# LP pooling in one dimension: one square and one sum per load, one root per store, and the small piece loaded second

## The chip, the cores and the metric

One core of a Trainium2 chip. ACT (ScalarE), DVE (VectorE) and SP (SyncE) are engines of the core that compute or issue transfers; 16 DMA engines move the data. The metric is the device time of one execution in microseconds (us). A kernel is compared by its runs in the same rounds on the same chip.

## The reference

```python
# x: 32 x 256 x 4096 float32, p = 2, kernel_size = 4
for i in range(out_length):                       # 1024
    window = np.abs(x[:, :, i*4:i*4+4]) ** p
    result[:, :, i] = (np.mean(window, axis=-1)) ** (1.0 / p)
```

With p = 2 this is a square, a sum over four neighbours, and a root with scale 1/4. The core reads 134.22 MB and writes 33.55 MB.

## The kernel before

x is taken as one flat array. 22 loads (18 of 13184 float32 columns on 128 partitions, then smaller ones) go into three slots, buffers that are used in turn. ACT squares each chunk in place, DVE sums groups of four, ACT takes the root, and a store follows for each group of loads. 840 columns per partition do not fit in this scheme. They form the **small piece**, 107,520 elements laid over 120 partitions, kept in a buffer that is not needed until later. A load is issued on SP's DMA queue as soon as its slot is free. The stores of groups 0 to 6 are issued on ACT's queue, those of groups 7 to 10 on SP's at the end.

```python
W, O_W = 13184, 6592
X_SLOTS, O_SLOTS = 3, 2
slots = [[(W, [4416, 4384, 4384])]] * 18          # width of a load, its chunks
slots += [[(6592, [3296, 3296])] * 2, [(6592, [3296, 3296]), (4216, [2112, 2104])]]
ODD = 840
groups = [2] * 9 + [3, 1]                         # loads to a store
FINE, ENDS, LAG = range(22), (), 1                # a root after every chunk
PAIRS = 16                                        # from this load on: packed adds
...
def total_sum(o, v, i):
    if i < PAIRS:
        nc.vector.tensor_reduce(out=o, in_=v.rearrange("p (n j) -> p n j", j=k), ...)
        return
    ...                                           # two adds: pairs, then pairs of pairs
    nc.vector.tensor_tensor(out=h, in0=q[:, :, 0:2], in1=q[:, :, 2:4], op=add)
    nc.vector.tensor_tensor(out=o, in0=h[:, :, 0], in1=h[:, :, 1], op=add)

Q = 120
odd = ODD * P // Q                                # 896 columns on 120 partitions
t = o_tiles[1][0:Q, 0:odd]
nc.sync.dma_start(out=t, in_=xf[(total - ODD) * P:total * P].rearrange("(p w) -> p w", p=Q))
...                                               # then loads 0, 1, 2
nc.scalar.activation(out=t, in_=t, func=Act.Square)
nc.vector.tensor_reduce(out=o, in_=..., op=mybir.AluOpType.add)
nc.scalar.activation(out=o, in_=o, func=Act.Sqrt, scale=1.0 / k)
nc.scalar.dma_start(out=of[...], in_=o)           # the small piece's store
...
for i in range(n):                                # for each chunk of each load:
    ...                                           # ACT squares, DVE sums, ACT roots
```

## Time and profile before

| | before |
|---|---|
| time, median of 3 runs | 394.59 us (394.59 to 394.62) |
| span of the profiled run | 392.8 us |
| bytes moved | 167.79 MB |
| busy: DMA, ACT, DVE | all but the two ends, 74%, 69% |

The prediction below shows the lines of the page and reads them. Two lines more are needed, from the timeline of the kernel before (start, length, engine, line, operation, tile; in brackets the idle time of the engine and what ended it). They show when loads 0 and 1 landed, since ACT stood waiting for them:

```profile
20.36 7.63 ACT L143 ACTIVATE xt<-xt 128x4416 f32<-128x4416 f32 x2 [12.97 <-DMA xt<-in_x_dram]
36.00 3.88 ACT L143 ACTIVATE xt<-xt 128x4416 f32<-128x4416 f32 x1 [1.06 <-DMA xt<-in_x_dram]
```

They started squaring at 20.36 and 36.00 us, 15.6 us apart, which is what 6.75 MB take at 433 GB/s.

### The profile page before, as it was taken

What the parts mean: (1) busy time and instruction counts of PE and PEld (TensorE: products, weight loads), DVE (VectorE), ACT (ScalarE), POOL (GpSimd) and SP (SyncE); (2) the same over time, 40 slices, a digit from 0 to 9 for tenths busy, and PEclk for the clock granted to TensorE, in tenths of its full rate; (3) what the DMA queues carried; (4) which work ended last, traced back from release to release, by engine and by line L of the source; (5) the groups of instructions that cost most, each with busy time, mean ns of one, the idle gap of its engine ahead of it and who ended that gap; (6) DMA issues with size and microseconds to landing.
All of it is one profiled execution on the core that took longest, in us unless ns stands there. A gap on an engine that the chain in (4) does not pass through costs nothing.

```text
span 392.8 us, 341 instructions
## 1 busy us (share of the span) xinstructions
DVE 271.8 (69%) x77; ACT 292.5 (74%) x128; POOL 0.2 (0%) x4
## 2 busy tenths in 40 slices
DVE  1059989594959495949594959495949494778781
ACT  3088987776776777677867786868586859899990
POOL 0000000000000000000000000000000000000000
DMA  9999999999999989999999999999999999999997
GB/s 361 420 429 446 446 446 384 430 470 430 389 432 473 430 387 435 467 430 422 432 435 430 427 435 427 430 435 459 459 404 430 459 438 430 395 430 432 429 432 315
DMA packets 5024, 167.79 MB, mean 427 GB/s; under 512 B 558, under 2 KB 678, under 8 KB 926
## 3 DMA queue, kind: packets, MB, share of 16 engines
q1 hardware_dynamic: 3879, 144.04, 85.2%
q10 hardware_dynamic: 1143, 23.73, 14.0%
q14 instruction: 2, 0.02, 0.0%
HBM read 134.22 MB, written 33.55 MB: 427 GB/s over the span
## 4 chain that ended last, share of the span: by engine, by line
DMA 62%; ACT 21%; DVE 10%; issue 4%; SPq 0%; ACTq 0%
DMA xt<-in_x_dram 62%; ACT xt L143 17%; DVE ot L96 8%; ACT ot L89 3%; ACT xt L89 1%; DVE xt L105 1%; DVE xt L106 0%; ACTq L86 0%; SPq L80 0%; SPq L112 0%; ACTq L89 0%
## 5 line engine op out<-in xcount | busy, mean ns | idle before, releaser
L143 ACT ACTIVATE xt<-xt 128x4384 f32<-128x4384 f32 (+4 forms) x62 | 229.6, 3705 | 85.1 <-DMA xt<-in_x_dram 81.9
L96 DVE TENSOR_REDUCE ot<-xt 128x1096 f32<-128x4384 f32 (+1 forms) x48 | 227.0, 4731 | 90.1 <-ACT xt L143 89.8
L89 ACT ACTIVATE ot<-ot 128x1096 f32<-128x1096 f32 (+1 forms) x54 | 59.8, 1107 | 1.8 <-DVE ot L96 1.1
L105 DVE TENSOR_TENSOR xt<-xt 128x1648 f32<-128x1648 f32 (+4 forms) x14 | 28.4, 2032 | 16.0 <-ACT xt L143 16.0
L89 ACT ACTIVATE xt<-xt 128x824 f32<-128x824 f32 (+2 forms) x8 | 6.5, 817 | 1.9 <-DVE xt L106 1.9
L106 DVE TENSOR_TENSOR ot<-xt 128x1096 f32<-128x1096 f32 (+1 forms) x6 | 7.8, 1303 | 0.2
L106 DVE TENSOR_TENSOR xt<-xt 128x824 f32<-128x824 f32 (+2 forms) x8 | 7.5, 939 | 0.3
L119 DVE TENSOR_REDUCE ot<-ot 120x224 f32<-120x896 f32 x1 | 1.1, 1086 | 5.7 <-ACT ot L117 5.7
L117 ACT ACTIVATE ot<-ot 120x896 f32<-120x896 f32 x1 | 0.9, 949 | 2.7 <-DMA ot<-in_x_dram 2.7
L117 ACT ACT_TABLE_LOAD x1 | 1.3, 1283 | 0.7 <-PEq L174 0.7
L123 ACT ACT_TABLE_LOAD x1 | 1.3, 1283 | 0.0
L123 ACT ACTIVATE ot<-ot 120x224 f32<-120x224 f32 x1 | 0.4, 389 | 0.0
L174 POOL MEMSET const-bfloat16-1.0<- 128x1 bf16 x1 | 0.1, 101 | 0.0
L174 POOL MEMSET const-uint8-127<- 128x1 uint8 x1 | 0.1, 101 | 0.0
L174 POOL MEMSET const-float32-0.0<- 128x1 f32 x1 | 0.1, 99 | 0.2 <-issue 0.2
L174 POOL MEMSET const-float32-1.0<- 128x1 f32 x1 | 0.1, 99 | 0.0
## 6 DMA issues: line engine op xcount, KB each, us to landing
xt<-in_x_dram SPq DMA_DIRECT2D x18, 6592.0 KB, 39.9
out_dram<-ot ACTq DMA_DIRECT2D x7, 3296.0 KB, 27.6
xt<-in_x_dram SPq DMA_DIRECT2D x3, 3296.0 KB, 29.4
out_dram<-ot SPq DMA_DIRECT2D x2, 3296.0 KB, 30.0
out_dram<-xt SPq DMA_DIRECT2D x1, 2472.0 KB, 10.4
xt<-in_x_dram SPq DMA_DIRECT2D x1, 2108.0 KB, 26.8
out_dram<-xt SPq DMA_DIRECT2D x1, 527.0 KB, 7.1
ot<-in_x_dram SPq DMA_DIRECT2D x1, 420.0 KB, 4.0
```

The lines of the kernel that those rows point to most:

```text
L89: nc.scalar.activation(out=o, in_=o, func=Act.Sqrt, scale=1.0 / k)
L96: nc.vector.tensor_reduce(out=o, in_=v.rearrange("p (n j) -> p n j", j=k), axis=mybir.AxisListType.X, op=add,)
L105: nc.vector.tensor_tensor(out=h, in0=q[:, :, 0:2], in1=q[:, :, 2:4], op=add)
L106: nc.vector.tensor_tensor(out=o, in0=h[:, :, 0], in1=h[:, :, 1], op=add)
L117: nc.scalar.activation(out=t, in_=t, func=Act.Square)
L119: nc.vector.tensor_reduce(out=o, in_=t.rearrange("p (n j) -> p n j", j=k), axis=mybir.AxisListType.X, op=mybir.AluOpType.add,)
L123: nc.scalar.activation(out=o, in_=o, func=Act.Sqrt, scale=1.0 / k)
L143: nc.scalar.activation(out=v, in_=v, func=Act.Square)
L174: nc = _bacc.Bacc("TRN2", target_bir_lowering=False, num_devices=1)
```

## The change

It makes work coarser: one square and one reduction for a whole load, one root for a whole store, which saves the fixed part of many instructions (the three squares of a load took 11.57 us in the profile before). The packed adds (two `tensor_tensor` adds in place of one reduction) begin one load earlier. Load 0 is issued first, so that the main stream starts at once; the small piece follows it, is squared on DVE instead of ACT, and is stored on SP's queue. The core of the diff:

```diff
-    slots = [[(W, [4416, 4384, 4384])]] * 18
-    slots += [[(6592, [3296, 3296])] * 2, [(6592, [3296, 3296]), (4216, [2112, 2104])]]
+    slots = [[(W, [W])]] * 17 + [[(W, [6592, 6592])]]
+    slots += [[(6592, [6592]), (6592, [6592])], [(6592, [6592]), (4216, [2112, 2104])]]
-    FINE, ENDS, LAG = range(22), (), 1
-    PAIRS = 16
+    FINE, ENDS, LAG = (), {19}, 1
+    PAIRS = 15
...
+    load(0)
+    nc.sync.dma_start(
+        out=odd_x, in_=xf[(total - ODD) * P:total * P].rearrange("(p w) -> p w", p=Q),
+    )
+    ahead = 1
...
+    def odd_sum():
+        nc.vector.tensor_tensor(out=odd_x, in0=odd_x, in1=odd_x, op=mybir.AluOpType.mult)
+        nc.vector.tensor_reduce(out=odd_o, ...)
+    def odd_root():
+        nc.scalar.activation(out=odd_o, in_=odd_o, func=Act.Sqrt, scale=1.0 / k)
+        nc.sync.dma_start(out=of[...], in_=odd_o)
...
             nc.scalar.activation(out=v, in_=v, func=Act.Square)
+            if i == 0 and c == 0:
+                odd_sum()
             total_sum(ots[g][:, summed:summed + step // k], v, i)
...
+            if i == 0 and c == 0:
+                odd_root()
```

More of the change, by code (lines that the diff above doesn't have):

```diff
@@ L110 @@
     odd = ODD * P // Q
-    t = o_tiles[1][0:Q, 0:odd]
-    nc.sync.dma_start(out=t, in_=xf[(total - ODD) * P:total * P].rearrange("(p w) -> p w", p=Q))
-    ahead = 0
+    odd_x = o_tiles[1][0:Q, 0:odd]
+    odd_o = o_tiles[1][0:Q, odd:odd + odd // k]
+    load(0)
[3 more added lines that the diff above has]
+    ahead = 1
     while ahead < n and loads[ahead][0] < X_SLOTS:
@@ L116 @@
         ahead += 1
-    nc.scalar.activation(out=t, in_=t, func=Act.Square)
-    o = o_tiles[1][0:Q, odd:odd + odd // k]
-    nc.vector.tensor_reduce(
-        out=o, in_=t.rearrange("p (n j) -> p n j", j=k),
-        axis=mybir.AxisListType.X, op=mybir.AluOpType.add,
-    )
-    nc.scalar.activation(out=o, in_=o, func=Act.Sqrt, scale=1.0 / k)
-    nc.scalar.dma_start(
-        out=of[(total - ODD) * P // k:total * P // k].rearrange("(p w) -> p w", p=Q), in_=o,
-    )
+    def odd_sum():
+        nc.vector.tensor_tensor(out=odd_x, in0=odd_x, in1=odd_x, op=mybir.AluOpType.mult)
+        nc.vector.tensor_reduce(
+            out=odd_o, in_=odd_x.rearrange("p (n j) -> p n j", j=k),
+            axis=mybir.AxisListType.X, op=mybir.AluOpType.add,
+        )
+    def odd_root():
+        nc.scalar.activation(out=odd_o, in_=odd_o, func=Act.Sqrt, scale=1.0 / k)
+        nc.sync.dma_start(
+            out=of[(total - ODD) * P // k:total * P // k].rearrange("(p w) -> p w", p=Q),
+            in_=odd_o,
+        )
     pending = []
```

## The prediction

> **What bounds the kernel now.** I read the page first: the slices in part 2, the costliest groups in part 5, and the chain of waits in part 4; then the windows view, the groups kept apart by shape, the waits of the SP queue and the timeline of the two ends.
>
> The slices and totals of the page:
>
> ```profile
> span 392.8 us, 341 instructions
> DVE 271.8 (69%) x77; ACT 292.5 (74%) x128; POOL 0.2 (0%) x4
> ...
> DMA  9999999999999989999999999999999999999997
> GB/s 361 420 429 446 446 446 384 430 470 430 389 432 473 430 387 435 467 430 422 432 435 430 427 435 427 430 435 459 459 404 430 459 438 430 395 430 432 429 432 315
> DMA packets 5024, 167.79 MB, mean 427 GB/s; under 512 B 558, under 2 KB 678, under 8 KB 926
> ```
>
> No compute engine is over 74%, while every slice of the DMA row except the last is 8 or 9. The windows view (length, DVE, ACT and POOL busy, clock, DMA share, GB/s) makes this sharper:
>
> ```profile
> 0.00:6.00 6.00, 0.28 (x1) 2.53 (x3) 0.20 (x4) 1.00 0.91 327
> 66.00:380.00 314.00, 229.38 (x65) 243.33 (x105) 0.00 (x0) 1.00 1.00 433
> 380.00:388.00 8.00, 3.09 (x4) 3.26 (x4) 0.00 (x0) 1.00 1.01 434
> ```
>
> For 314 us the 16 DMA engines are busy 100% at 433 GB/s, and still while the last roots are computed. At 433 GB/s, 167.79 MB take 387.5 us, so of the span of 392.8 only 5.3 us are anything else: the start before the first byte, a slow first few us, and the landing of the last store. The time of 394.59 us is the span plus 1.8. Arithmetic matters only if it lets the transfer queues run dry. The chain of waits (DMA 62%, ACT 21%, DVE 10%) misleads here: it steps through an ACT or DVE instruction because a load's issue waits for a slot, but that load then stands in line behind other loads. Its landing takes 39.9 us (part 6) although its 6.75 MB need only 15.6 us at 433 GB/s.
>
> [...] The trace runs at 433 to 434[...], so I take 434 as the wall. [...] each load lands behind the one before, and the stores on the ACT queue take 27.6 us where 3.38 MB alone need 7.8. [...]
>
> **The change part by part.** The rows I extrapolate from, kept apart by shape (count | busy us, mean ns | idle before):
>
> ```profile
> L96 DVE TENSOR_REDUCE ot<-xt 128x1096 f32<-128x4384 f32 x32 | 151.0, 4719 | 6.3 <-ACT xt L143 6.0
> L143 ACT ACTIVATE xt<-xt 128x4384 f32<-128x4384 f32 x36 | 138.4, 3843 | 3.3 <-ACT ot L89 3.3
> L89 ACT ACTIVATE ot<-ot 128x1096 f32<-128x1096 f32 x36 | 39.7, 1103 | 0.2
> L105 DVE TENSOR_TENSOR xt<-xt 128x1648 f32<-128x1648 f32 x6 | 11.3, 1875 | 3.9 <-ACT xt L143 3.8
> L105 DVE TENSOR_TENSOR xt<-xt 128x2192 f32<-128x2192 f32 x4 | 9.8, 2442 | 3.9 <-ACT xt L143 3.9
> ```
>
> Bytes: none removed, none added. This part is worth 0.
>
> Work on the engines: the slope of the adds is (2442-1875)/(2192-1648) = 1.042 ns per element. One square of 13184 columns is 3.84 + 8800 x 0.833 ns = 11.2 us (three were 11.6); one reduction is 4.72 + 8800 x 1.042 ns = 13.9 us (three were 14.2); one root of 6592 columns is 1.10 + 5496 x 0.833 ns = 5.7 us (six were 6.6). ACT loses roughly 1.4 us per two loads and DVE 0.6, about 12 and 6 us over the kernel, all beside the transfers: worth 0. Load 15 now uses packed adds, 7.0 + 3.6 = 10.6 us: also 0.
>
> Depth of the pipeline: this is the cost. A slot used to be free 18.7 us after landing (51.58 to 70.31 in the chain), because the chunks' squares and sums overlap. Now square and sum of a whole load run in sequence, 11.2 + 13.9 = 25.1 us, so the next load of that slot is issued 6.4 us later. What it must beat is the landing of the two loads already queued: 2 x 15.6 = 31.2 us without a store, 38.9 with one (13.5 + 3.38 MB at 434). My count at the tightest place (loads counted from 0): load 1 lands at 36.0 (the square before it finished by 31), its square ends at 47.2, its sum at 61.1; load 4 is issued then, and load 3 drains until 67.2. About 6 us remain, later some 14. So no gap. DVE needs 13.9 us per load and ACT 11.2 + 5.7/2 = 14.0, both below 15.6 even with no stores.
>
> Stores: the root of a group now follows a whole square, so a store is issued 17 us after the even load lands instead of 5 (56.50 against 51.55). Its buffer is written again about 33 us after that (load 4's square ends near 101.7, the store is issued near 68.9); with 27 to 28 us to land, some 4 to 5 us remain.
>
> The head: before, SP issues the small piece at 0.73 and load 0 at 1.24; the piece lands at 4.72 and the first 6 us run at 327 GB/s instead of 434. With load 0 first the small rows lie between big ones; I estimate a gain of 0.3 to 0.8 us. Square and table load of the small piece move off ACT's start, where nothing waited. The small store on SP is held until about 31.7, and load 3 is not wanted before 43.9: 0.
>
> The tail. Before:
>
> ```profile
> 376.98 1.95 ACT L143 ACTIVATE xt<-xt 128x2112 f32<-128x2112 f32 x1
> 380.26 4.88 SPq L86 DMA_DIRECT2D out_dram<-xt  x2
> 384.15 0.64 ACT L89 ACTIVATE xt<-xt 128x526 f32<-128x526 f32 x1 [1.53 <-DVE xt L106]
> ```
>
> The last stores are issued at 380.26 and 384.81, and before them two full stores from SP end at 384.7. From load 17's landing at 340.6, chaining the new durations on ACT (two squares 11.3, square of 18 5.7, root 5.7, squares of 19 and 20 11.3, root 2.9, square 1.9, a wait of 0.7 for DVE, root 1.6) gives the second to last store at 381.5 and the last at about 386.4, so 1.2 and 1.6 us later. The transfers ahead end between 383 and 384, and an issue needs about 1 us to its first byte: it just fits. If load 16's square and root run past 340.6, it is 1.3 us later still and the queue is empty for up to 0.7 us. I charge 0.2.
>
> Sum: 394.59 + 0 - 0.5 (head) + 0.2 (tail) = 394.3; I say 394.3.
>
> **The rivals.**
> Rival 1, the whole-load latency starves the queue: if a slot is freed later than I count, each missed deadline idles all DMA engines. For it: slack of only 6 us at loads 3 and 4, and two output buffers with 4 to 5. Against: every duration is a short extrapolation along measured slopes, the wait would heal once stores lengthen the period to 38.9 us, and a one-time miss of 2 us would make 396 to 397. A miss in every period would be needed for over 402.
> Rival 2, the tail becomes the bound: the chunks in the last loads are twice as long, so the pipeline drains later. For it: ACT is nearly continuously busy from 340.6 on and the last two stores have under 1 us of slack. It would make 395 to 397.
> Rival 3, fewer instructions make it faster: 12 us of ACT and 6 of DVE are saved. Against: DMA is at 1.00 share of the time; the floor by bytes is 386.6 us at 434 plus about 2 at the front, 1.5 at the back and 1.8 outside the span, 392. So faster by over 2% (under 386.7) is ruled out by the bytes, unless the wall itself moves.
>
> **Range and chances.** The head's gain bounds the low side at about 393.3; a late tail and one small gap set the high side at 396.3. Over 2% slower needs about 8 us of empty queue, which only a recurring stall gives: 2%. Faster 1%, same 97%.
>
> **What would show it right or wrong.** In the changed profile: squares near 11.2 us, reductions near 13.9, roots near 5.7; SP's fourth load issued near 44 and its fifth near 61, both before the queue runs out; a DMA share of 1.00 at 433 from 6 to 380 us; first load landed near 19 instead of 20.3, and the third still near 51; last stores issued near 381.5 and 386.4. It is wrong if any window in the middle falls below 1.00, if DVE reductions wait for a store, or if the final store is issued after 389.

What is cut out of the prediction are figures and rules that no trace or run of this case shows. No term of its sum is cut: 394.59 - 0.5 (head) + 0.2 (tail) = 394.3 us. What stays rests on the trace of the kernel before. 434 GB/s is the rate of its window from 380 to 388 us, and the 314 us before that ran at 433; that this is a wall is the author's estimate. Loads 0, 1 and 2 landed one behind the other, at 20.34, 35.97 and 51.56 us. The 0.833 ns per element of ACT are (3843 - 1103) / (4384 - 1096) from the rows shown, and the 1.042 ns of the adds fit the reductions too: (4719 - 1086) / (4384 - 896), the 1086 ns being the small piece's. The "about 1 us" from an issue to its first byte is that of the small piece, issued at 0.73 us with its first row at 1.75; the last row of the run ends at 391.4 of 392.8 us, which are the "1.5 at the back". The gain at the head is an estimate from 327 against 434 GB/s; that large rows hide the cost of small ones was not shown.

## The result and the profile after

| | before | after |
|---|---|---|
| time, median of 6 runs | 394.61 us (394.59 to 394.63) | 395.66 us (395.55 to 396.12) |
| ratio, fast runs | | 1.0028 (95%: 1.0015 to 1.0041) |
| span of the profiled run | 392.8 us | 394.0 us |
| busy ACT, DVE | 292.5, 271.8 us | 280.9, 262.9 us |
| last load landed | 369.12 us | 370.26 us |
| last store landed | 391.91 us | 393.09 us |

A ratio is the mean time of one kernel's fast runs over that of the other's of the same rounds, so not quite the ratio of the medians. The time is the same within 2%, and about 1 us longer. ACT lost 11.6 us of work, about as foretold, and DVE 8.9, and it bought nothing. The totals and the slices of the page after:

```profile
span 394.0 us, 200 instructions
DVE 262.9 (67%) x35; ACT 280.9 (71%) x39; POOL 0.2 (0%) x4
...
DMA  8999999999999999999999999999999999999997
```

The groups kept apart by shape (count | busy us, mean ns | idle before, and what ended it) give the new durations:

```profile
L96 DVE TENSOR_REDUCE ot<-xt 128x3296 f32<-128x13184 f32 x15 | 208.3, 13886 | 78.9 <-ACT xt L152 78.9
L152 ACT ACTIVATE xt<-xt 128x13184 f32<-128x13184 f32 x17 | 190.2, 11190 | 102.4 <-DMA xt<-in_x_dram 100.7 <-ACT ot L89 1.7
L89 ACT ACTIVATE ot<-ot 128x6592 f32<-128x6592 f32 x9 | 51.1, 5681 | 0.0
```

11.19, 13.89 and 5.68 us: the extrapolation along the slopes was right to the rounding. DVE waits for squares (78.9 and 22.1 us) and for the small piece (22.0), and never for a store, so the two output buffers suffice. Now the windows (length, DVE, ACT and POOL busy, clock, DMA share, GB/s), first the middle and the last stores:

```profile
66.00:380.00 314.00, 226.27 (x27) 237.70 (x30) 0.00 (x0) 1.00 1.00 432
380.00:388.00 8.00, 4.85 (x5) 4.83 (x4) 0.00 (x0) 1.00 0.99 427
```

The DMA engines are never out of work. The 1.2 us must be somewhere the share does not show: the engines are busy, and slower. The landings tell where. The timeline of the kernel after:

```profile
20.13 11.19 ACT L152 ACTIVATE xt<-xt 128x13184 f32<-128x13184 f32 x1 [18.12 <-DMA xt<-in_x_dram]
...
37.39 11.19 ACT L152 ACTIVATE xt<-xt 128x13184 f32<-128x13184 f32 x1 [4.37 <-DMA xt<-in_x_dram]
...
45.26 70.48 SPq L80 DMA_DIRECT2D xt<-in_x_dram  x5
```

Load 0 lands 0.23 us sooner than before, although nothing is ahead of it now. Load 1 lands 1.39 us later, although the same bytes have been read by then. Load 3 is issued at 45.26 us, long before load 2 lands at 52.95, so no lateness of slots is in it. From here the shift stays: 1.40 us at load 2, 1.14 at the last load, 1.18 at the last store. So all of it arises between loads 0 and 1, where the small piece now lies. The windows of that stretch, before and after:

```profile
16.00:24.00 8.00, 0.00 (x0) 3.64 (x1) 0.00 (x0) 1.00 1.00 430
```

```profile
16.00:24.00 8.00, 1.94 (x2) 3.87 (x1) 0.00 (x0) 1.00 1.01 370
```

The same busy share, 1.00 and 1.01, but 370 GB/s instead of 430: (430 - 370) x 8 us is 480 KB, or 1.1 us at 433.

The trace also records every row that a DMA engine moved. The usual time of a 52,736-byte row is 1947 ns, 27.1 GB/s for an engine. I add up, over all rows of a stretch, the time beyond bytes at 27.1 GB/s and divide by 16 engines. This makes the table that the rest is read from (us; the last two columns are when the 16 engines finished the last store, on average and the latest):

| kernel | 0-8 | 8-26 | 54-80 | whole run | mean end | latest end |
|---|---|---|---|---|---|---|
| before | 0.94 | 0.08 | 0.49 | 2.47 | 390.58 | 391.41 |
| after | 0.83 | **1.29** | 0.06 | 3.35 | 391.44 | 392.58 |

0.88 us more of slow rows, and the engines end 0.86 us later on average. The remaining 0.3 us is one engine that ends 1.14 us behind the mean instead of 0.83.

### The profile page after: what moved, and what is told of

Its sections match the earlier page's. It is cut to its first block, busy times and chain, and to the rows that moved or that the text cites. A ratio compares the mean times of both kernels' runs of the same rounds, so it can differ in the third digit from the quotient of the medians.

```text
span 394.0 us, 200 instructions
## 1 busy us (share of the span) xinstructions
DVE 262.9 (67%) x35; ACT 280.9 (71%) x39; POOL 0.2 (0%) x4
## 4 chain that ended last, share of the span: by engine, by line
DMA 44%; ACT 29%; DVE 16%; issue 8%; another core or an unknown queue 1%; ACTq 0%; SPq 0%
DMA xt<-in_x_dram 44%; ACT xt L152 23%; DVE ot L96 14%; ACT ot L89 6%; DVE xt L105 1%; ACT xt L89 1%; DVE xt L106 1%; ACTq L86 0%; SPq L114 0%; SPq L80 0%; ACTq L89 0%
## 5 line engine op out<-in xcount | busy, mean ns | idle before, releaser
L152 ACT ACTIVATE xt<-xt 128x13184 f32<-128x13184 f32 (+3 forms) x24 | 222.2, 9272 | 103.1 <-DMA xt<-in_x_dram 101.4
L96 DVE TENSOR_REDUCE ot<-xt 128x3296 f32<-128x13184 f32 x15 | 208.3, 13886 | 78.9 <-ACT xt L152 78.9
L89 ACT ACTIVATE ot<-ot 128x6592 f32<-128x6592 f32 x9 | 51.1, 5681 | 0.0
L105 DVE TENSOR_TENSOR xt<-xt 128x3296 f32<-128x3296 f32 (+3 forms) x9 | 34.5, 3835 | 22.4 <-ACT xt L152 22.1
L123 DVE TENSOR_TENSOR ot<-ot 120x896 f32<-120x896 f32 x1 | 1.1, 1093 | 22.0 <-DMA ot<-in_x_dram 22.0
L106 DVE TENSOR_TENSOR ot<-xt 128x3296 f32<-128x3296 f32 (+1 forms) x4 | 10.9, 2733 | 0.1
L89 ACT ACTIVATE xt<-xt 128x3296 f32<-128x3296 f32 (+2 forms) x3 | 5.6, 1870 | 2.8 <-DVE xt L106 2.8
L106 DVE TENSOR_TENSOR xt<-xt 128x1648 f32<-128x1648 f32 (+2 forms) x5 | 7.0, 1409 | 0.2
L124 DVE TENSOR_REDUCE ot<-ot 120x224 f32<-120x896 f32 x1 | 1.1, 1086 | 0.0
## 6 DMA issues: line engine op xcount, KB each, us to landing
ot<-in_x_dram SPq DMA_DIRECT2D x1, 420.0 KB, 20.8
```

The costliest lines, as they stand in the source:

```text
L123: nc.vector.tensor_tensor(out=odd_x, in0=odd_x, in1=odd_x, op=mybir.AluOpType.mult)
L124: nc.vector.tensor_reduce(out=odd_o, in_=odd_x.rearrange("p (n j) -> p n j", j=k), axis=mybir.AxisListType.X, op=mybir.AluOpType.add,)
L152: nc.scalar.activation(out=v, in_=v, func=Act.Square)
```

## The experiments

Twelve kernels ran. Those of one group shared a chip and the runs of the kernel before.

**First group: is it the place of the small piece (theory A) or the coarse work (theory B)?** The kernel before took 394.69 us here.

*The piece in first place again, all else as changed:*

```diff
-    load(0)
     nc.sync.dma_start(out=odd_x, ...)
+    load(0)
```

> The changed kernel with one thing undone: the small piece is again loaded ahead of load 0 (its arithmetic and its store stay as changed). Theory A (the small rows behind a full load make every DMA engine start slowly a second time, and that alone costs the 1.1 us): 394.5 us +-0.2, ratio to the kernel before 0.9995 to 1.0005, load 1 lands near 36.0 us instead of 37.4. Theory B (whole-load squares and sums, later issues and later stores cost it, the place of the piece is innocent): stays at 395.5 to 395.8.

Measured: 394.61 us (394.19 to 395.55), ratio 1.0003 (0.9990 to 1.0016). Load 1 lands in time:

```profile
35.77 11.19 ACT L152 ACTIVATE xt<-xt 128x13184 f32<-128x13184 f32 x1 [2.69 <-DMA xt<-in_x_dram]
```

The coarse work is all there and the median is that of the kernel before: A's number, not B's. But the runs scatter over 1.4 us, where the kernel before scatters over 0.5, and two of the five (395.48 and 395.55) are as slow as B would have them, so B is not out; the last part comes back to it. The profiled one took 395.48: its slow rows sum to 2.48 us as before, its mean end is 390.62, but one engine ended at 392.11, 1.49 us behind.

*The kernel before, with load 0 ahead of the piece:*

```diff
-    nc.sync.dma_start(out=t, ...)
-    ahead = 0
+    load(0)
+    nc.sync.dma_start(out=t, ...)
+    ahead = 1
```

> The kernel before with one thing done: load 0 is issued ahead of the small piece; chunks, roots and sums as before. Theory A: 395.5 to 395.9 us, load 1 lands near 37.3. Theory B: stays at 394.6 +-0.1.

Measured: 395.51 us (395.24 to 396.53), ratio 1.0024 (1.0011 to 1.0038). Its window:

```profile
16.00:24.00 8.00, 0.00 (x0) 0.90 (x1) 0.00 (x0) 1.00 1.03 350
```

350 GB/s, 1.77 us of slow rows between 8 and 26 us, mean end 391.91 (the profiled run took 396.32 us; load 1 landed at 38.61, later than written). The order of two lines is enough to make the kernel before as slow as the changed one. (ACT's first square waits here for the piece until 23.1 us; load 3 is still issued at 44.81, before load 2 lands at 54.25.)

*The piece behind all three first loads:*

```diff
-    load(0)
-    nc.sync.dma_start(out=odd_x, ...)
-    ahead = 1
+    ahead = 0
     while ahead < n and loads[ahead][0] < X_SLOTS:
         load(ahead)
         ahead += 1
+    nc.sync.dma_start(out=odd_x, ...)
```

> The changed kernel with the small piece behind all three first loads instead of behind load 0. Theory A: the second slow start is merely moved, so 395.3 to 395.8 us again, with load 1 near 36 and load 2 near 51.5 us but load 3 late by 1 to 1.5 us. A variant of A, that it hurts only right behind the first load where the engines are still out of step: 394.4 to 394.6. Theory B: 395.6.

Measured: 415.47 us, ratio 1.0526. A fault of my edit, and a lesson: the piece's sum stands ahead of load 0's in DVE's program, so DVE waited 52.5 us for the piece while load 0 lay squared. No slot was freed, and the transfers ran dry:

```profile
52.00:70.00 18.00, 17.45 (x4) 15.23 (x3) 0.00 (x0) 1.00 0.16 47
```

47 GB/s instead of 433 for 18 us loses 16 of the 20.8 us. This run tells nothing of A and B, but it shows what a dry queue looks like, and that the changed kernel has none.

*No piece at all: its columns are added to the last load.*

```diff
-    slots += [..., [(6592, [6592]), (4216, [2112, 2104])]]
-    ODD = 840
+    slots += [..., [(6592, [6592]), (5056, [2528, 2528])]]
+    ODD = 0
```

(and the piece's instructions removed)

> The changed kernel without a small piece: its 840 columns a partition are added to the last load (5056 columns, two chunks of 2528), same bytes. Theory A: neither the small rows nor a second slow start remain, 393.6 to 394.3 us. Theory B: 395.2 to 395.6, as the coarse work is all still there. The last store should be issued near 387.6 us.

Measured: 395.58 us (395.26 to 395.85), ratio 1.0021. A miss for A's number. The stretch from 8 to 26 us is clean (0.01 us), as A says, but 0.86 us of slow rows turn up between 54 and 80 us, where the first store starts, against 0.49 before and 0.06 in the changed kernel; and one engine ended 1.56 us behind the mean. So taking the piece away removes its slow rows, and the time stays. The larger part of what takes their place is that engine: against the kernel before, the mean end is 0.16 us later and the latest end 0.88.

**Second group: what about the piece is slow?** The kernel before took 394.64 us here. A1: a run of small rows is slow by itself. A2: 15 of 16 engines get a share, and being out of step costs. (In the trace of the changed kernel 15 completions of the piece come from 20.17 to 22.01 us and one at 1.76, when the first row of load 0 only starts; load 0 on 128 partitions has 16 from 18.29 to 20.10.)

*128 partitions instead of 120, still second:*

```diff
-    Q = 120
+    Q = 128
```

> The changed kernel with the small piece on 128 partitions (rows of 3360 bytes, all 16 DMA engines) instead of 120 (3584 bytes, 15 engines), still in second place. Theory A1 (a run of small rows behind big ones is what costs, whoever carries it): 395.4 to 395.9 us, as the change. Theory A2 (the engine that gets no share of the piece runs ahead and the others pay for being out of step): 394.5 to 394.9.

Measured: 395.40 us (395.11 to 395.61), ratio 1.0017. The number is A1's, but the trace refutes A1:

```profile
16.00:24.00 8.00, 2.06 (x2) 4.41 (x1) 0.00 (x0) 1.00 1.06 456
```

All 128 small rows took 132 ns, 25 GB/s for an engine, and no large row of this stretch took over 1992 ns; in the changed kernel 120 rows took 212 ns on average and large rows up to 2912. On 128 partitions the piece brings next to no slow rows (0.10 us from 8 to 26). Again the first store costs instead: 0.79 us from 54 to 80.

*The piece's load on ACT's queue, in the changed kernel and in the kernel before:*

```diff
-    nc.sync.dma_start(out=odd_x, ...)
+    nc.scalar.dma_start(out=odd_x, ...)
```

> The changed kernel with the load of the small piece issued on ACT's queue instead of SP's, at the same time as load 0. Its small rows then take turns with load 0's big ones instead of coming as one run after them. Theory A1 (a run of small rows pays the latency of each row and makes the big rows behind it start slowly): 394.0 to 394.7 us, load 1 lands near 36.0. If the cost sticks to the piece wherever it comes: 395.4 to 395.9.

Measured: 396.76 us (396.34 to 396.96), ratio 1.0050.

> The kernel before with the load of its small piece on ACT's queue and nothing else changed. Under A1 the 0.55 us of slow small rows at the head lie beside load 0's rows: 394.0 to 394.6 us; if small rows cost the same anywhere: 394.6 to 394.8.

Measured: 396.25 us (395.96 to 396.96), ratio 1.0042. Both misses, and the most telling ones. The small rows take turns with load 0's large ones from 4 to 22 us. They are fairly quick themselves (157 and 159 ns), but now nearly every large row beside them is slow: in the first of the two, the large rows begun before 7.5 us had a median of 2238 ns, against 1949 in the changed kernel, and those begun from 16 to 24 us one of 2198. The window of the first:

```profile
6.00:16.00 10.00, 0.00 (x0) 0.00 (x0) 0.00 (x0) 1.00 0.97 365
```

Slow rows add up to 3.09 us from 0 to 26 in the first and 3.13 in the second. So the piece slows its neighbours, and the longer it lies beside them, the more. A1 falls: its small rows were to be hidden by this. The small load on ACT's queue made the changed kernel 1.1 us slower (396.76 against 395.66, each beside the same 394.6 of the kernel before), and the kernel before 1.6 us (396.25 against 394.64).

*The piece late, between loads 19 and 20, with nothing waiting for it:*

```diff
-    odd_x = o_tiles[1][0:Q, 0:odd]
+    odd_x = x_tiles[1][0:Q, 10808:10808 + odd]
...
+            if ahead == 20:
+                nc.sync.dma_start(out=odd_x, ...)
             load(ahead)
...
-            if i == 0 and c == 0:
+            if i == 19 and c == 0:
...
     store(g, nc.sync)
+    if g == 8:
+        nc.sync.dma_start(out=of[...], in_=odd_o)
```

> The changed kernel with the small piece loaded late, between loads 19 and 20, into free columns of a load slot; its sum on DVE and its root on ACT follow the square of load 19, its store goes between two late stores. Made so that nothing waits for it, which the run with the piece in fourth place did not manage. Theory A1 (small rows between big ones cost wherever they are): 395.2 to 396.3 us, with some 0.4 of it from the root on ACT's tail. If it hurts only near the start: 394.3 to 395.0.

Measured: 398.37 us (398.05 to 398.55), ratio 1.0093: worse than expected. The window where it lands:

```profile
351.00:360.00 9.00, 8.80 (x4) 9.00 (x3) 0.00 (x0) 1.00 0.99 320
```

320 GB/s for 9 us at a full DMA share, against 431 in the changed kernel: 2.3 us at 433. The slow rows of this window alone sum to 2.28 us. So it is no matter of the start; the piece slows whatever runs beside it, at the end as well. By then the engines were 2.3 us out of step; whether it cost more here for that, no run tests.

**Third group: fewer than 128 partitions, or an uneven share?** The kernel before took 394.62 us here. Theory P: a piece that is not laid over 128 partitions slows its own rows and those beside it, even if every engine has a share. The rival, theory E: the uneven share alone (the trace shows 15 completions at the end of a transfer over 120 partitions, and 16 for 128 or 64).

*64 partitions: 16 completions, so each engine has a share, but half of the partitions:*

```diff
-    Q = 120
+    Q = 64
```

> The changed kernel with the small piece on 64 partitions (rows of 6720 bytes[...]), in second place. Theory P[...]: its rows take clearly longer than the 248 ns their bytes need at 27.1 GB/s an engine, the big rows around them are slow too, and the time is 395.4 to 396.5 us. Theory E (only the uneven share, 15 engines of 16, is what hurts): rows near 250 ns, no slow big rows beside them, as the run on 128 partitions, 395.0 to 395.4.

Measured: 396.24 us (395.94 to 396.34), ratio 1.0040.

```profile
16.00:24.00 8.00, 1.02 (x1) 3.34 (x1) 0.00 (x0) 1.00 1.04 350
```

The median small row took 494 ns (the mean 420), twice the 248 that 6720 bytes take at 27.1 GB/s, and large rows begun in this stretch took up to 3579. 1.86 us of slow rows from 8 to 26. No engine is without a share here, and the rows are slow all the same, so E alone falls, and P is borne out as far as it goes. Why fewer partitions are slow was not shown: the trace does not name a row's engine. A row's length changes along with the partitions here; by itself it is no likely cause, since the median row of 4216, 16,864, 26,368 and 52,736 bytes took within 8% of the time at 27.1 GB/s.

*128 partitions and first place, in the changed kernel:*

```diff
-    Q = 120
+    Q = 128
...
-    load(0)
     nc.sync.dma_start(out=odd_x, ...)
+    load(0)
```

> The changed kernel with the small piece on 128 partitions and in first place[...]. Theory P: its rows take about 132 ns; 394.0 to 394.6 us, unless the slow big rows at the first store, which the run on 128 partitions in second place and the run without a piece both showed (0.8 us), come back: then 395.0 to 395.4.

Measured: 395.59 us (394.78 to 395.62), ratio 1.0019. The second branch of what was written, and 0.2 us above it: the piece costs little (0.58 us from 0 to 8, 0.08 from 8 to 26), the first store 0.73.

*The kernel before on 128 partitions:*

```diff
-    Q = 120
+    Q = 128
```

> The kernel before with its small piece on 128 partitions instead of 120 and nothing else: the candidate that would beat both. Theory P: its rows fall from 205 to about 132 ns, 0.5 us less over the engines, so 394.0 to 394.3 us; with a larger first-store cost 394.5 to 394.9.

Measured: 394.67 us (394.51 to 394.95), ratio 1.0002. The head falls from 0.94 to 0.52 us, the first store rises from 0.49 to 0.79. No gain: no version that ran beats both kernels. The last two runs make a pair: in both the piece is first and on 128 partitions, their slow rows are alike (0.73 and 0.79 us at the first store), and one has coarse work and the other fine. Yet the coarse one is 0.9 us slower: four of its five runs lie above all five of the other. Its mean end is 0.22 us later, its latest end 0.99.

*The piece's store back on ACT's queue, in the changed kernel:*

```diff
-        nc.sync.dma_start(out=of[...], in_=odd_o)
+        nc.scalar.dma_start(out=of[...], in_=odd_o)
```

> The changed kernel with the store of the small piece back on ACT's queue. All theories: the queue of this store is innocent, 395.5 to 395.9 us; the transfer then runs beside load 1 or 2 instead of behind load 2, and ACT loses about 0.6 us where it has time to spare.

Measured: 395.95 us (395.73 to 396.34), ratio 1.0037 (1.0023 to 1.0051), which overlaps with the 1.0028 (1.0015 to 1.0041) of the change; the median lies just above what was expected. The queue of this store is innocent, and the slow rows of the changed kernel come again (1.24 us from 8 to 26).

The table of slow rows for these runs, without the one that ran dry:

| kernel | 0-8 | 8-26 | 54-80 | whole run | mean end | latest end |
|---|---|---|---|---|---|---|
| after, piece first | 1.00 | 0.04 | 0.35 | 2.48 | 390.62 | 392.11 |
| before, piece second | 0.81 | 1.77 | 0.06 | 3.76 | 391.91 | 393.12 |
| after, no piece | 0.71 | 0.01 | 0.86 | 2.55 | 390.74 | 392.29 |
| after, 128 second | 0.84 | 0.10 | 0.79 | 2.76 | 390.80 | 391.93 |
| after, ACT's queue | 1.22 | 1.87 | 0.05 | 4.30 | 392.37 | 393.61 |
| before, ACT's queue | 1.27 | 1.86 | 0.06 | 4.31 | 392.39 | 393.05 |
| after, piece late | 0.77 | 0.06 | 0.88 | 5.08 | 393.26 | 394.95 |
| after, 64 second | 0.80 | 1.86 | 0.06 | 3.81 | 391.88 | 392.97 |
| after, 128 first | 0.58 | 0.08 | 0.73 | 2.66 | 390.76 | 392.30 |
| before, 128 | 0.52 | 0.16 | 0.79 | 2.45 | 390.54 | 391.31 |
| after, store on ACT's queue | 0.77 | 1.24 | 0.05 | 3.19 | 391.27 | 392.29 |

In every row the mean end less the whole run's slow rows is 388.0 to 388.2 us. The slow rows thus account for the mean end in all of them, with coarse work or fine. This is bookkeeping of engines that are never idle; it does not say why a row is slow. What the slow rows do not account for is how far the latest engine lies behind, 0.7 to 1.7 us.

## Why the prediction was right, and where it was not

The measured 395.66 lies within 393.3 to 396.3, and the class, within 2%, had 97%. It is 1.36 us above the 394.3, and the direction was wrong: 0.3 us faster was said, and the kernel is 1.05 us slower. The high side of the range stood for a late tail and a small gap in the queue, and neither came; that it also covers a loss at the head, which was not foreseen, is luck. By its steps:

- **What bounds the kernel**: right. The share stays 1.00 at 432 GB/s in the middle. ACT and DVE lost 20 us of work together and the time did not fall, which is rival 3's end.
- **Work on the engines**: right to the rounding, 11.19, 13.89, 5.68 us, and the two adds 7.03 + 3.59 for 7.0 + 3.6. ACT saved 11.6 us for about 12 (by luck: the durations shown make 1.7 us per two loads, not 1.4, and some of that was overlap of neighbouring instructions, which busy time does not count twice: ACT's groups sum to 299.9 us before for 292.5 busy, and to 281.9 after for 280.9); DVE 8.9 for about 6, as the gain of load 15's packed adds (10.6 for 14.2 us) was not counted.
- **Depth of the pipeline**: right. Load 3 was issued at 45.26 (foretold near 44) and load 4 at 62.52 (near 61). Load 3 landed at 68.82, so 6.3 us remained of the 6 counted. Rival 1 did not come about.
- **Stores**: right. No DVE instruction waited for a store.
- **The tail**: right in substance. The last two stores were issued at 382.65 and 387.64, 1.15 and 1.24 us later than foretold, by as much as all loads were late (the durations listed sum to 381.7, not 381.5). Between the last load and the last store the tail added 0.04 us; 0.2 was charged. Rival 2 did not come about in the profiled run:

```profile
382.65 5.32 SPq L86 DMA_DIRECT2D out_dram<-xt  x2
```

- **The head**: this step failed. "With load 0 first the small rows lie between big ones; I estimate a gain of 0.3 to 0.8 us." It took the 327 GB/s of the first 6 us for a cost of the small rows that large rows beside them would hide. First, most of the slow start is not theirs: in the changed kernel the first 16 rows are large ones, and they take 2213 to 3204 ns instead of 1947. The slow rows from 0 to 8 us fall only from 0.94 to 0.83 us, and to 0.71 without any piece, so there was little to gain. Second, on 120 partitions the small rows slow the large ones beside them: 1.29 us from 8 to 26. Load 0 does land "near 19" where the piece is not right behind it (piece in fourth place):

```profile
19.35 11.19 ACT L151 ACTIVATE xt<-xt 128x13184 f32<-128x13184 f32 x1 [17.35 <-DMA xt<-in_x_dram]
```

With the piece behind it, load 0 landed at 20.10 us, 0.24 sooner than before instead of 1.3. Load 1 came 1.39 us later than before, and load 2 at 52.95, not "still near 51". Of the places tried for the 120-partition piece, first place, where no large row is beside it yet, was the best. Moving the piece back gave a median of 394.61 us, and moving it in the kernel before gave 395.51.

With the shift of 1.14 us at the last load in place of -0.5 for the head, and 0.04 in place of 0.2 for the tail, the sum is 394.59 + 1.18 = 395.77; the profiled run took 395.79. The two shifts are measured in that run, so this checks that no step is missing, and no more.

**What stays open.** First, the slow rows where the first store starts. They come to 0.35 to 0.88 us in the kernels whose first loads ran undisturbed, and to 0.05 or 0.06 wherever the piece had disturbed them between 8 and 26 us. Why the first store costs so little where the piece had cost before, no run shows. Second, the latest engine: in the changed kernel and its variants it is 1.0 to 1.7 us behind the mean; in the kernel before 0.83, and 0.7 to 1.2 in its variants. In the profiled run with the piece first, the latest engine fell back by 1.0 us between 146 and 168 us, while four rows took about 0.25 us longer each; what slowed them is not in the trace.

So theory B is not dead. Curing the piece in the changed kernel (128 partitions in either place, or no piece) gave only 395.40 to 395.59 us. The first store does not explain this, since the kernel before on 128 partitions pays as much there and takes 394.67. The latest engine does in the main (0.7 us without a piece and with 128 first, but only 0.3 with 128 second). In the four coarse kernels with the least slow rows from 8 to 26 us (piece first, no piece, piece late, 128 first) it ends 1.5 to 1.7 us behind the mean, against 1.1 with the piece second on 128 partitions (0.10 us of slow rows there), and 0.8 in the kernel before and in that on 128 partitions. In all four it falls back by 0.5 to 0.9 us between the landings of loads 7 and 8; in these two fine ones no step before load 15 is above 0.25. What the coarse work does to that engine is not in the trace, and three of the five runs with the piece first (394.19 to 394.61) show no loss. In the change itself the piece is the larger part: 0.86 us of the 1.17 by which the latest end moved are the mean of all engines, and 0.31 the latest one.

## What to carry to other kernels

When the DMA engines are the bound, read the GB/s beside the share: engines can be fully busy and slow (370 GB/s at a share of 1.01 here, 430 at 1.00 before), and landing times of equal loads show where. A transfer that does not span all 128 partitions took time from those beside it here (1.2 to 1.9 us of slow rows on 120 and 64, when it came second), so try it where nothing runs beside it, or over 128, and measure: over 128 the slow rows went, but the kernel did not become faster. And an instruction that waits for a late transfer must not stand ahead of work that frees a slot: that cost 20 us here.
